# Cached keys and values of a head pair: load and split placed behind the pair's first key or value projection step

## The chip, the core and the metric

The kernel runs on one core of a Trainium2 chip. The metric is device time in microseconds (us) of one execution. The core has a matmul engine (TensorE, PE in the profile, with its weight loads as PEld), VectorE (DVE), ScalarE (ACT), GpSimd (POOL) and SyncE (SP), whose queue issues all the transfers of this kernel.

## The reference, cut to what matters

Two encoder layers are computed for 1024 prompt frames and 64 sample frames that share their weights. The sample frames also attend to 256 cached frames.

```python
# even layer, group B: 8 heads of chunk-band attention (group A is latent attention)
kb_all = jnp.concatenate([c_bk, k_b], 1); vb_all = jnp.concatenate([c_bv, v_b], 1)
o_b = _band_sample(q_b, kb_all, vb_all, c_bk.shape[1], table)
# odd layer: 16 heads of stick-breaking attention
q, k, v = _odd_project(x, w_in)
k_all = jnp.concatenate([c_k, k], 1); v_all = jnp.concatenate([c_v, v], 1)
o = _stick_breaking(q, k_all, v_all, pos, jnp.arange(k_all.shape[1]))
return o.reshape(B, T, MIX_C) @ w_out, k, v      # k and v are outputs too
# every layer: x <- LN(alpha*x + mixer(x)); x <- LN(alpha*x + sqrelu_mlp(x))
```

## The kernel before, in words

All products are made to float32 accuracy from two parts of each operand: `split` (L151) writes a high part H with ACT (L152) and the remainder L with DVE (L153); `mm3` then makes three matmuls (L157 to L159) for one product. Heads are handled in pairs, since a head has 64 features: four pairs of the band attention in the even layer, eight pairs in the odd one. `heads64` (L568) sets up one pair. Its nine steps project queries, keys and values for the token chunks 0:384, 384:768 and 768:1088, each with 24 matmuls into one PSUM bank ("d" or "s", two of each; from the second pair on only the two "d"). A key step is copied out of its bank by `split` for either head of the pair into the tile kS (64 partitions each), and by one more ACT copy (L618) into a tile `kraw`, which is stored to the output (L620). In the odd layer every key step has that copy, in the band layer only the steps from token 512 on; a value step has it always, and its `kraw` is then transposed and split into V (`put_values`, L538). The bank is free when the last of these copies has read it. `kraw` has two buffers, used in turn by all that asks for it.

The cached keys and values of the pair go the same way: a load into a `kraw` tile (L586 keys, L593 values, 128 KB), in the band layer a store of that tile to an output (L588, L595), and `split` into columns 1024:1280 of kS (one ACT and one DVE instruction for either head) or into blocks 8 and 9 of V (one of each). This stands at the head of the first "k" and the first "v" step, behind the load and split of the projection weight (`weight`, L183) and ahead of the 24 matmuls. The cached rows are read by the fifth of the nine work units of the pair's attention (`attend`, L813; `order` holds a pair (0, 4) there).

The attention of a pair runs beside the projection of the next: `paced` (L641) ties each projection step to a transpose of the running attention. In attention, scores (L655) go to a bank; in the odd layer ACT makes two sigmoids (L713, L714), DVE a scan (L720, L722) and POOL a product (L723); the weights are transposed (L175), split into wtH and wtL, and multiplied with V (L787, L789). The first pair of either layer has its nine steps ahead of any attention; in the odd layer they are taken in the order k0, q0, k1, q1, k2, q2, v0, v1, v2.

The order of the instructions in each engine's queue is not that of the source. The framework plans it ahead of time on a timeline of its own estimates: an instruction that stands earlier in the source has the higher priority, but one whose operands are planned to be ready is placed when its engine is free. On the chip each queue then runs in the planned order, and the head of a queue that waits for a semaphore holds up what stands behind it.

Of the kernel before, what the change touches and what calls it, by code (L numbers as in the profile page):

```python
# [13 lines left out]
P = 128  # L14
D = 1024
KD = D // P
SEQ = 1024
DEC = 64
T = SEQ + DEC
PAST = 256  # L20
# [24 lines left out]
def key_parts(c0, n):  # L45
    if c0 + n <= SEQ:
        return [(0, n, c0)]
    a = SEQ - c0
    return [(0, a, c0), (a, n - a, SEQ + PAST)]
# [74 lines left out]
class Net:  # L124
# [443 lines left out]
    def heads64(self, cp, bp, tiles, pair, w, cacheT, cache_v, outs, out0, cache_outs=(None, None), first=None, sooner=None, order=None):  # L568

        nc = self.nc
        qH, qL, qS, kS, V = tiles
        half = (slice(0, 64), slice(64, 128))
        feat = slice(pair * P, (pair + 1) * P)
        x = (self.xH, self.xL)
        ws = {}

        def step(kind, c0, n):
            if kind not in ws:
                ws[kind] = first if kind == "k" and first else self.weight(w[kind][pair], [P, KD, P], sooner)
                if kind == "k":
                    raw = self.tl(bp, [P, 384], "kraw", 2)
                    nc.sync.dma_start(raw[:, :PAST], cacheT[pair])  # L586
                    if cache_outs[0] is not None:
                        nc.sync.dma_start(cache_outs[0][feat, :], raw[:, :PAST])  # L588
                    for h in range(2):
                        self.split(kS[half[h], h, SEQ : SEQ + PAST], kS[half[1 - h], h, SEQ : SEQ + PAST], raw[half[h], :PAST])  # L590
                if kind == "v":
                    raw = self.tl(bp, [P, 2, P], "kraw", 2)
                    nc.sync.dma_start(raw, cache_v[:, feat].rearrange("(b p) c -> p b c", p=P))  # L593
                    if cache_outs[1] is not None:
                        nc.sync.dma_start(cache_outs[1][:, feat].rearrange("(b p) c -> p b c", p=P), raw)  # L595
                    self.split(V[:, 8:10, :, :64], V[:, 8:10, :, 64:], raw.rearrange("p b (h d) -> p b h d", h=2))
            ps = self.ps("d" if pair else "ds")
            mark = self.dense(ps[:, :n], ws[kind], x, KD, c0, n)
            if kind == "q":
                m = min(n, SEQ - c0)  # L600
                for h in range(2):
                    r, c = half[h], slice(c0, c0 + m)
                    self.split(qH[r, h, c], qL[r, h, c], ps[r, :m])
                    nc.scalar.activation(qH[half[1 - h], h, c], ps[r, :m], AF.Copy)
                    if m < n:
                        c = slice(h * DEC, h * DEC + DEC)
                        self.split(qS[r, h, 0, c], qS[r, h, 1, c], ps[r, m:n])
                        nc.scalar.activation(qS[half[1 - h], h, 0, c], ps[r, m:n], AF.Copy)  # L608
                return mark
            if kind == "k":  # L610
                for a, m, kc in key_parts(c0, n):
                    for h in range(2):
                        r, c = half[h], slice(kc, kc + m)
                        self.split(kS[r, h, c], kS[half[1 - h], h, c], ps[r, a : a + m])
            lo = max(c0, out0)
            if lo < c0 + n or kind == "v":
                raw = self.tl(bp, [P, 384], "kraw", 2)
                nc.scalar.activation(raw[:, :n], ps[:, :n], AF.Copy)  # L618
                if lo < c0 + n:
                    nc.sync.dma_start(outs[kind][feat, lo - out0 : c0 + n - out0], raw[:, lo - c0 : n])  # L620
                if kind == "v":
                    parts = [(i * P, min(P, n - i * P), (c0 // P + i) if c0 + i * P < SEQ else 10) for i in range(-(-n // P))]
                    self.put_values(V, raw, parts)
            return mark

        work = [(kind, c0, n) for kind in "kqv" for c0, n in CHUNKS]
        if order:
            work = [work[i] for i in order]
        steps = [lambda a=a: step(*a) for a in work]

        def score(h, i):

            if i < 8:
                st = [(x[:, h, i * P : i * P + P], kS[:, h, :]) for x in (qH, qL)]
            else:
                st = [(qS[:, e, x, :], kS[:, e, :]) for e in range(2) for x in range(2)]
            return lambda kc, n: self.scores([(a, k[:, kc : kc + n]) for a, k in st], n)

        return score, V, steps
# [1206 lines left out]
```

## Time and profile before

| | |
|---|---|
| time, median of 3 runs | 2795.22 us (2793.05 to 2797.9) |
| profiled execution: its time, its span | 2797.55 us, 2795.8 us |
| mean granted TensorE clock | 0.992 |
| busy share of the span: PE, DVE, ACT, POOL | 98%, 77%, 54%, 27% |
| band attention and its projections | about 177 to 400 us |
| first pair's projections of the odd layer | about 1428 to 1472 us |
| stick-breaking attention of the odd layer | about 1472 to 1955 us |

Busy times are those of one execution. A pause of PE that the profile lists has behind it, in brackets, its length and what ended it. Matmuls overlap, so the start-to-start distance of two matmuls, and not the duration of one, is what a matmul costs.

### The profile page before, as it was taken

The numbers are of one execution on the slowest core, as the hardware profiler recorded it, in microseconds if no ns is written. First come the engines' busy times: TensorE is split into PE (matmuls) and PEld (weight loads), VectorE is DVE, ScalarE is ACT, GpSimd is POOL, SyncE is SP. The second block draws the span as 40 slices with busy tenths as digits, with TensorE's granted clock in tenths as the row PEclk, the third lists the DMA queues.
The fourth block names the chain that finished last, engine by engine and source line by source line (L and its number), as shares of the span: only waits on it lengthen the run. The fifth ranks groups of instructions, "written<-read, shape, count | busy, mean of one in ns | idle before, by whom it ended". The sixth has DMA issues, their size and how long they took to land. (4 is left out here: it accounts for less than half of the span.)

```text
span 2795.8 us, 46944 instructions
## 1 busy us (share of the span) xinstructions
PE 2728.2 (98%) x16931; PEld 2496.0 (89%) x16931; DVE 2158.9 (77%) x3833; ACT 1511.5 (54%) x3103; POOL 745.6 (27%) x879
## 2 busy tenths in 40 slices
PE   9999999999999999999999999999999999999998
PEld 8999987888999998888789999998789999977786
DVE  4336777786867777999968887878787777789999
ACT  4235666873555556333257777777545555543331
POOL 3123334652100001221533343434330000022245
PEclk9999999989999999999999999999999999999999
DMA  7152234334234448444321111112252444763432
GB/s 216 49 168 60 73 97 100 87 108 149 93 131 139 162 143 268 131 139 138 111 91 58 51 54 52 54 51 80 77 168 100 161 131 138 242 189 120 150 122 87
DMA packets 226801, 331.33 MB, mean 119 GB/s; under 512 B 44489, under 2 KB 159241, under 8 KB 226505
## 3 DMA queue, kind: packets, MB, share of 16 engines
q1 hardware_dynamic: 226568, 328.34, 37.1%
q8 instruction: 134, 2.20, 0.3%
q14 instruction: 99, 0.80, 0.1%
HBM read 216.58 MB, written 109.99 MB: 117 GB/s over the span
## 5 line engine op out<-in xcount | busy, mean ns | idle before, releaser
L723 POOL TENSOR_TENSOR G<-G,S 128x384 f32<-128x384 f32 (+4 forms) x200 | 201.2, 1010 | 339.6 <-DVE S L720 121.2
L157 PE MATMUL d<-xH,wH 128*128 128x384 f32 (+1 forms) x784 | 262.6, 335 | 3.8 <-ACT qS L608 2.3
L159 PE MATMUL d<-xH,wL 128*128 128x384 f32 (+1 forms) x784 | 261.4, 333 | 0.0
L158 PE MATMUL d<-xL,wH 128*128 128x384 f32 (+1 forms) x784 | 260.1, 332 | 0.0
L153 DVE TENSOR_TENSOR wtL<-t,wtH 128x512 fp32r<-128x512 f32 (+2 forms) x328 | 196.9, 618 | 46.3 <-ACT wtH L152 37.5
L152 ACT ACTIVATE wtH<-t 128x512 fp32r<-128x512 f32 (+2 forms) x328 | 170.3, 545 | 47.9 <-PE t L175 21.3
L1493 POOL MEMSET sl<- 64x1024 f32 x2 | 1.9, 948 | 661.7 <-PE d L158 331.0
L787 PE MATMUL pv<-wtH,V 128*128 128x256 f32 (+1 forms) x624 | 159.2, 280 | 4.0 <-ACT o L747 2.8
L662 POOL TENSOR_TENSOR R<-R,inv 128x640 f32<-128x640 f32 (+6 forms) x100 | 115.5, 1167 | 174.8 <-DVE inv L661 103.5
L789 PE MATMUL pv<-wtL,V 128*128 128x256 f32 (+1 forms) x624 | 154.2, 288 | 7.5 <-DVE wtL L153 7.4
L157 PEld LDWEIGHTS d<-xH,wH 128*128 128x128 f32 x784 | 147.9, 189 | 8.1 <-ACT qS L608 3.2
L720 DVE TENSOR_TENSOR_SCAN S<-S,own 128x513 f32<-128x513 f32 (+3 forms) x144 | 144.3, 1012 | 11.9 <-ACT S L713 9.7
L158 PEld LDWEIGHTS d<-xL,wH 128*128 128x128 f32 x784 | 147.9, 189 | 1.3
L159 PEld LDWEIGHTS d<-xH,wL 128*128 128x128 f32 x784 | 147.7, 188 | 1.2
L152 ACT ACTIVATE wo<-wo 128x1024 fp32r<-128x1024 f32 (+4 forms) x92 | 79.7, 875 | 103.4 <-DMA wo<-o 24.9
L789 PEld LDWEIGHTS pv<-wtL,V 128*128 128x128 f32 x624 | 120.4, 193 | 11.3 <-DVE wtL L153 9.9
L787 PEld LDWEIGHTS pv<-wtH,V 128*128 128x128 f32 x624 | 120.1, 192 | 9.5 <-ACT o L747 5.6
L175 PE MATMUL t<-ident,G 128*128 128x128 f32 x600 | 103.3, 277 | 13.5 <-POOL S L711 7.7
L655 PE MATMUL s<-kS,qH 128*128 128x384 f32 (+3 forms) x288 | 105.7, 369 | 3.3 <-DVE mx L678 2.3
L713 ACT ACTIVATE S<-s 128x384 f32<-128x384 f32 (+4 forms) x200 | 98.7, 494 | 14.4 <-PE s L655 12.5
L714 ACT ACTIVATE G<-s 128x384 f32<-128x384 f32 (+4 forms) x200 | 99.5, 497 | 0.1
L655 PE MATMUL s<-kS,qL 128*128 128x384 f32 (+3 forms) x288 | 96.9, 338 | 0.0
(1817 smaller groups left out, 9906.3 us busy)
## 6 DMA issues: line engine op xcount, KB each, us to landing
sl<-a_d SPq DMA_DIRECT2D x37, 512.0 KB
wo<-a_d SPq DMA_DIRECT2D x36, 512.0 KB
a_d<-wo SPq DMA_DIRECT2D x31, 544.0 KB
wo<-in_w_dn SPq DMA_DIRECT2D x27, 512.0 KB
wo<-in_w_up SPq DMA_DIRECT2D x21, 512.0 KB
a_d<-sl SPq DMA_DIRECT2D x19, 544.0 KB
sl<-in_w_dn SPq DMA_DIRECT2D x20, 512.0 KB
sl<-in_w_up SPq DMA_DIRECT2D x17, 512.0 KB
```

The lines of the kernel that those rows point to most:

```text
L152: self.after(self.nc.scalar.activation(H, src, AF.Copy), mark)
L153: (engine or self.nc.vector).tensor_tensor(L, src, H.bitcast(F32), op=ALU.subtract)
L157: i = mm(out, aH, bH, start=first, stop=False)
L158: mm(out, aH, bL, start=False, stop=False)
L159: mm(out, aL, bH, start=False, stop=last)
L175: return self.nc.tensor.transpose(out, in_, self.ident[:n, :n])
L655: self.nc.tensor.matmul(ps[:, :n], q, k, start=i == 0, stop=i == len(passes) - 1)
L662: nc.gpsimd.tensor_tensor(R[:, :nk], R[:, :nk], inv.to_broadcast([P, nk]), op=ALU.mult)
L720: nc.vector.tensor_tensor_scan(s[r], s[r], own, carry, op0=ALU.mult, op1=ALU.max)
L723: nc.gpsimd.tensor_tensor(G[:, :n], G[:, :n], S[:, 1 : n + 1], op=ALU.mult)
L787: mm(out, v, wH[:, s : s + n], start=bi == 0 and s == 0, stop=False)
L789: mm(out, v, wL[:, s - n : s], start=False, stop=bi == len(banks) - 1 and j == bank[-1][0])
```

## The change

The load, the store and the split of the cached rows become a function `cached`. The step calls it behind its product instead of ahead of it, and only for the chunk that starts at token 0. Since `product` contains the copies out of the bank, the cached rows now stand behind the whole first key step (its splits, its L618 copy and its store), and behind the whole first value step (its L618 copy, its store and `put_values`). The amount of work is the same. The turn of the two `kraw` buffers changes: in an odd pair the uses were cached keys, k0, k1, k2, cached values, v0, v1, v2, and become k0, cached keys, k1, k2, v0, cached values, v1, v2.

```diff
+        def cached(kind):
+            if kind == "k":
+                raw = self.tl(bp, [P, 384], "kraw", 2)
+                nc.sync.dma_start(raw[:, :PAST], cacheT[pair])
+                if cache_outs[0] is not None:
+                    nc.sync.dma_start(cache_outs[0][feat, :], raw[:, :PAST])
+                for h in range(2):
+                    self.split(kS[half[h], h, SEQ : SEQ + PAST], kS[half[1 - h], h, SEQ : SEQ + PAST], raw[half[h], :PAST])
+            if kind == "v":
+                raw = self.tl(bp, [P, 2, P], "kraw", 2)
+                nc.sync.dma_start(raw, cache_v[:, feat].rearrange("(b p) c -> p b c", p=P))
+                if cache_outs[1] is not None:
+                    nc.sync.dma_start(cache_outs[1][:, feat].rearrange("(b p) c -> p b c", p=P), raw)
+                self.split(V[:, 8:10, :, :64], V[:, 8:10, :, 64:], raw.rearrange("p b (h d) -> p b h d", h=2))
+
         def step(kind, c0, n):
+            mark = product(kind, c0, n)
+            if c0 == 0:
+                cached(kind)
+            return mark
+
+        def product(kind, c0, n):
             if kind not in ws:
                 ws[kind] = first if kind == "k" and first else self.weight(w[kind][pair], [P, KD, P], sooner)
-                if kind == "k":
...
-                if kind == "v":
...
             ps = self.ps("d" if pair else "ds")
             mark = self.dense(ps[:, :n], ws[kind], x, KD, c0, n)
```

## Rows read from the trace of the kernel before

**Rows 1.** The page, busy time of each engine over the whole span.
```profile
PE 2728.2 (98%) x16931; PEld 2496.0 (89%) x16931; DVE 2158.9 (77%) x3833; ACT 1511.5 (54%) x3103; POOL 745.6 (27%) x879
```

**Rows 2.** Stretches: from:to, length, busy of PE, PEld, DVE, ACT, POOL, clock, DMA.
```profile
177.00:400.00 223.00, 220.20 (x1485) 217.66 (x1484) 139.31 (x437) 140.03 (x340) 73.56 (x87) 0.99 0.25 77
...
1490.00:1945.00 455.00, 439.07 (x2968) 422.54 (x2967) 380.41 (x550) 335.61 (x805) 179.74 (x347) 1.00 0.16 50
```

**Rows 3.** Waits of PE from 1440 to 1950: total us, times, longest us.
```profile
PE t L175 <- POOL S L711: 5.3, 9, 1.3
PE pv L789 <- DVE wtL L153: 5.1, 5, 1.1
PE d L157 <- ACT qS L608: 2.3, 3, 0.9
...
PE s L157 <- ACT kraw L618: 1.8, 1, 1.8
```

**Rows 4.** What touches kraw: durations min/median/max in ns, first and last start.
```profile
L153 DVE TENSOR_TENSOR kS<-kraw,kS x24: 407/420/747, 190.1 to 1886.9; 64x256 fp32r<-64x256 f32 x24
...
L153 DVE TENSOR_TENSOR V<-kraw,V x12: 391/426/1018, 201.2 to 1909.8; 128x256 fp32r<-128x256 f32 x12
```

**Rows 5.** Timeline of PE, first odd pair, every third matmul of k2: start, duration.
```profile
1447.37 0.41 PE L157 MATMUL s<-xH,wH 128*128 128x320 f32 x1 [1.81 <-ACT kraw L618]
...
1447.92 0.33 PE L157 MATMUL s<-xH,wH 128*128 128x320 f32 x1
...
1451.65 0.31 PE L157 MATMUL s<-xH,wH 128*128 128x320 f32 x1
...
1452.09 0.31 PE L157 MATMUL s<-xH,wH 128*128 128x320 f32 x1
```

**Rows 6.** Stretches of 2 us behind that pause, columns as in rows 2.
```profile
1448.00:1450.00 2.00, 2.00 (x10) 2.00 (x9) 0.56 (x1) 1.34 (x4) 0.23 (x4) 0.52 0.55 197
1450.00:1452.00 2.00, 2.00 (x11) 2.00 (x10) 0.00 (x0) 0.47 (x1) 0.00 (x0) 0.63 0.03 8
```

**Rows 7.** Timeline of ACT, the same place.
```profile
1443.68 0.86 ACT L152 ACTIVATE kS<-kraw 64x256 fp32r<-64x256 f32 x2 [0.31 <-DMA kraw<-in_cache_skT]
1444.56 0.49 ACT L152 ACTIVATE kS<-s 64x384 fp32r<-64x384 f32 x1
...
1446.85 0.47 ACT L618 ACTIVATE kraw<-s 128x384 f32<-128x384 f32 x1
```

**Rows 8.** Timeline of DVE, the same place.
```profile
1444.28 0.55 DVE L153 TENSOR_TENSOR kS<-s,kS 64x384 fp32r<-64x384 f32 x1
1444.76 0.86 DVE L153 TENSOR_TENSOR kS<-kraw,kS 64x256 fp32r<-64x256 f32 x2
1445.65 0.56 DVE L153 TENSOR_TENSOR kS<-s,kS 64x384 fp32r<-64x384 f32 x1
```

**Rows 9.** Timeline of SP: a load of the first odd pair, two stores of a later one.
```profile
1441.60 0.33 SPq L586 DMA_DIRECT2D kraw<-in_cache_skT  x1
...
1591.48 6.68 SPq L620 DMA_DIRECT2D o_svT<-kraw  x2
```

**Rows 10.** Timeline of DVE, cached keys of the third odd pair.
```profile
1548.27 0.75 DVE L153 TENSOR_TENSOR kS<-kraw,kS 64x256 fp32r<-64x256 f32 x1
1549.05 0.56 DVE L153 TENSOR_TENSOR wtL<-t,wtH 128x384 fp32r<-128x384 f32 x1
```

**Rows 11.** Timeline of PE, the same place.
```profile
1549.66 0.39 PE L789 MATMUL pv<-wtL,V 128*128 128x256 f32 x1 [0.80 <-DVE wtL L153]
```

**Rows 12.** Timeline of POOL, the same place.
```profile
1547.50 1.24 POOL L723 TENSOR_TENSOR G<-G,S 128x512 f32<-128x512 f32 x1 [1.25 <-DVE S L722]
```

**Rows 13.** Timeline of ACT, first band pair.
```profile
189.66 0.86 ACT L152 ACTIVATE kS<-kraw 64x256 fp32r<-64x256 f32 x2 [7.79 <-DMA kraw<-in_cache_bkT]
```

**Rows 14.** Stretches of one odd pair each, columns as in rows 2.
```profile
1540.00:1609.00 69.00, 65.27 (x436) 62.06 (x435) 56.26 (x83) 48.97 (x117) 26.91 (x51) 1.00 0.18 54
1609.00:1676.00 67.00, 65.33 (x445) 63.20 (x443) 57.82 (x83) 51.10 (x123) 26.58 (x52) 1.00 0.17 54
```

More of the change, by code (lines that the diff above doesn't have):

```diff
@@ L579, in heads64 @@
         ws = {}
-        def step(kind, c0, n):
+        def cached(kind):
[12 more added lines that the diff above has]
+                self.split(V[:, 8:10, :, :64], V[:, 8:10, :, 64:], raw.rearrange("p b (h d) -> p b h d", h=2))
+        def step(kind, c0, n):
+            mark = product(kind, c0, n)
[3 more added lines that the diff above has]
+        def product(kind, c0, n):
             if kind not in ws:
                 ws[kind] = first if kind == "k" and first else self.weight(w[kind][pair], [P, KD, P], sooner)
-                if kind == "k":
[L585 to L590, printed above, removed]
-                if kind == "v":
[L592 to L596, printed above, removed]
             ps = self.ps("d" if pair else "ds")
```

## The prediction

> **What bounds the kernel now.** The page's first part comes first: PE is busy 2728.2 us of 2795.8 us [rows 1]. So 67.6 us is all that any shift of work between the other engines can win at once, apart from a higher clock. The moved work lies in two stretches. Tabled as stretches, they show where PE stands still: in the band layer 223.00 - 220.20 = 2.8 us, in the stick-breaking layer from 1490 to 1945 us 455.00 - 439.07 = 15.9 us, with DVE at 380.41 of 455 us and ACT at 335.61 [rows 2]. PE sets the pace; DVE, five sixths full, is the engine that makes PE wait.
>
> The waits of PE say for whom: POOL's memsets, DVE's wtL, the query copies, and once, for 1.8 us, the copy L618 of a key step [rows 3]. No line names a cached load or split. The cached rows can therefore matter only as something that stands in a queue ahead of what PE waits for, and the timelines have to show where they do. The list for kraw gives their cost: 24 key pieces on DVE at 0.420 us and 12 value pieces at 0.426 us [rows 4], with ACT pieces of about the same length. That makes 24 moved groups, a key and a value group in each of 12 pairs.
>
> **The change part by part.** *First odd pair, where a moved group stands in front of PE.* Step k2 needs the bank of k0 and starts after a pause of 1.81 us, ended by k0's L618 [rows 5]. Behind the pause the granted clock is 0.52 and then 0.63 of full speed [rows 6], so part of the time is at the lower level of 1.2 GHz. The starts of k2's L157 show what that costs: from 1447.92 to 1451.65 five groups of three matmuls take 3.73 us, where the next group takes 0.44 us [rows 5], so 3.73 - 5 x 0.44 = 1.53 us are lost.
>
> L618 is late because the copies out of k0's bank alternate between ACT and DVE, and the cached keys stand between them on both. On ACT the two cached pieces (0.31 us of waiting for the load, then 0.86 us) precede the split of k0's second head at 1444.56 [rows 7]. On DVE the two cached pieces fill 1444.76 to 1445.62, and k0's second head follows at 1445.65 [rows 8]. With the cached pieces behind L618, ACT can begin that second head at 1443.68; DVE, at work on k1's first head until 1444.28 + 0.55 = 1444.83, then takes it for 0.56 us until 1445.4; and L618 follows, ending at about 1445.9 instead of 1446.85 + 0.47 = 1447.3. Gain 1.4 us. The pause left is 0.4 us. Pauses of up to 1.3 us are among those between 1490 and 1945 [rows 3], where the granted clock is 1.00 [rows 2], so I take the 1.53 us as won too. Bounds: nothing, if the planner fits the cached pieces into gaps of the same chain, and 1.81 + 1.53 = 3.3 us, if the whole pause goes. I take 1.4 + 1.5 = 2.9 us, since the removed work (1.17 us on ACT, 0.86 us on DVE) is in the chain itself.
>
> *The load.* Here it goes from issue at 1441.60 [rows 9] to its first use at 1443.68 [rows 7] in 2.08 us. In an odd pair the load moves past one issue of SP, k0's store (keys) or v0's store (values), each about 0.33 us; what stands behind it, weight loads above all, is later by no more than the wait for that copy. The fifth attention unit, first to read the cached rows, belongs to the next pair period, some 67 us on. I cost it at nothing. If that cover were gone it would cost its 2.08 us.
>
> *The turn of the kraw buffers.* k1 now takes k0's buffer and waits for its store to land. With the load's 2.08 us for a store, k1's copy cannot start before 1445.9 + 2.1 = 1448.0; its bank is next wanted by v0, behind k2 and q2 of 8 x 0.44 = 3.5 us each, from 1446 on, so at 1453. v1 likewise takes over v0's buffer two uses later; in a later pair two value stores are issued within 6.68 us [rows 9], against 2.08 us for landing plus the transposes of v0. Nothing; bound 2.1 us at the first pairs, whose steps have no attention between them.
>
> *The other 22 odd and band groups beside this pair's.* Their work (two pieces or one of 0.42 us on either engine) is the same before and after; only its neighbours differ. Of these groups one stops PE in the trace: the third odd pair's second key piece ends at 1549.02, the split wtL follows [rows 10] and PE has waited 0.80 us for it [rows 11]. That pause may go, and another may come. I take one such pause before and one after, so 0; bounds -0.8 us and, if each group met a wtL, 22 x 0.80 = +17.6 us. Where a group is hidden it is hidden under PE's matmuls, and costs 0.80 us when it is not.
>
> That piece took 0.75 us instead of 0.42 us, and ran while POOL multiplied from 1547.50 to 1548.74 [rows 12]. The Trainium skill (page SBUF — State Buffer, section Who interferes with whom) says that a VectorE instruction with two SBUF inputs contends with a GpSimd instruction that reads SBUF; the trace agrees here, with 0.33 us more. By that rule the copies out of a bank are spared and the cached pieces are not, so that a piece moved onto a POOL product would add an estimated 0.33 us to a pause; by the rows alone the price stays 0.80 us.
>
> *First band pair.* ACT waits 7.79 us at the head of its queue for the cached load [rows 13], ahead of k0's second head. It looks like the largest prize. But the band stretch holds 2.8 us of PE pauses in all, and none is ended by this: four banks serve this pair. Gain 0.
>
> *Sum.* -1.4 - 1.5 = -2.9 us: against the profiled execution 2797.55 - 2.9 = 2794.65 us. That execution lies 2.33 us above the median of the three runs, so the forecast is 2795.22 - 2.9 = 2792.3 us. Below, 0.2% of the time, 5.6 us, is what a measurement can tell from no change.
>
> **The rivals.**
>
> *Nothing moves.* Queue order is planned by readiness. If the cached pieces are planned into the same gaps as now, the time is 2795.2 us. For it: two buffers of kraw are free at the start of the odd layer, so the load can still be planned at 1441.6. Against it: in ACT's queue the cached pieces would have to precede a split that is ready by the same moment and now has priority.
>
> *A better rhythm.* Odd pairs alternate: 69.00 - 65.27 = 3.7 us of pauses in one, 67.00 - 65.33 = 1.7 us in the next [rows 14]. If that holds for the six pairs from 1540 on, three are long, and they could become short if later cached pieces and earlier L618 copies unload DVE at the right moment: 3 x 2.0 = 6 us more, 2795.2 - 2.9 - 6 = 2786.3 us. For it: the pauses are DVE's, and banks are freed sooner. Against it: the largest part of the pauses, 5.3 us, is ended by POOL's memsets [rows 3], which the change doesn't touch.
>
> *Slower: cached pieces ahead of wtL.* At their new place the pieces hold up wtL as in the third pair, 0.80 us each time. With all seven later odd pairs and three band pairs hit by their keys it is 10 x 0.8 - 2.9 = +5.1 us, 2800.3 us; from (5.6 + 2.9) / 0.8 = 11 groups on it is measurably slower, with all 22 it is 2809.9 us. For it: DVE is at 380 of 455 us. Against it: it happens in 1 of 22 now.
>
> **How the numbers follow.** The forecast has 0.38, nothing moves 0.18, the better rhythm 0.27, slower 0.17. The first two lie within 0.2%, but the forecast can miss it by a little: faster 0.29, same 0.54, slower 0.17. The range from 2785.5 to 2800.5 us takes in the better rhythm with a margin of 0.8 us and the ten hits; the likeliest case alone spans 2790 to 2795 us.
>
> **What would show it.** In the first odd pair: L618 of k0 ahead of the pieces from kraw on ACT and DVE, k2's pause under 0.8 us, granted clock 1.00 from 1448 to 1452. In the later pairs: the waits of PE for wtL at about the 5.1 us of now. In the first band pair: ACT's long wait gone or moved, with PE unchanged. The prediction is wrong if k2's pause stays (planned gaps), if PE's waits for wtL or for POOL change by more than 3 us over the odd layer, or if the projections wait for kraw buffers.

## The result and the profile after

The changed kernel takes 2808.88 us (median of 4 runs, 2806.34 to 2813.55) against 2794.75 us before, measured on the same chip. The ratio is 1.005, with a 95% interval of 1.0038 to 1.0062. The forecast was 2792.3 us with a range up to 2800.5 us: the change is slower by 14 us, where no change or a gain of 3 us was expected. The profiled execution spans 2811.8 us. In the changed kernel the lines behind the edit are numbered nine higher: L618 is now L627, L711 L720, L714 L723, L723 L732, L655 L664, L789 L798.

The span is 16.0 us longer, but PE is busy only 6.3 us longer than in [rows 1], and it does the same products: most of the loss has to be found in its pauses. The page's first part:

```profile
PE 2734.5 (97%) x16931; PEld 2499.0 (89%) x16931; DVE 2163.2 (77%) x3833; ACT 1509.0 (54%) x3103; POOL 752.1 (27%) x879
```

The two stretches of [rows 2] again, from the view of stretches (PE, PEld, DVE, ACT, POOL busy, granted clock, DMA share, GB/s). The odd layer begins 6.0 us later here (memset of `own` at 1447.6 instead of 1441.6 us), so the second stretch holds slightly earlier work than in [rows 2]:

```profile
177.00:400.00 223.00, 219.54 (x1472) 216.78 (x1472) 139.41 (x435) 140.03 (x337) 73.27 (x87) 0.99 0.26 78
1490.00:1945.00 455.00, 433.04 (x2887) 413.59 (x2886) 379.43 (x540) 326.26 (x788) 173.63 (x336) 1.00 0.16 49
```

In the stick-breaking stretch PE now pauses 455.00 - 433.04 = 22.0 us instead of 15.9 us and gets through 2887 matmul records instead of 2968. The waits of PE from 1440 to 1950 us (total us, times, longest) say for whom:

```profile
PE d L157 <- ACT kraw L627: 6.8, 7, 1.2
PE s L664 <- ACT G L723: 4.2, 4, 1.3
PE t L175 <- POOL G L732: 4.0, 9, 0.7
PE t L175 <- POOL S L720: 2.7, 5, 1.3
PE pv L798 <- DVE wtL L153: 2.5, 3, 1.4
PE t L175 <- DVE V L153: 0.9, 2, 0.4
PE s L157 <- ACT kraw L627: 0.6, 1, 0.6
```

The first line is new: a projection step waits for the copy L627 out of a bank, seven times about 1 us. From 1480 to 1960 us this line was 0.8 us in two waits before. The waits for POOL's memsets and for wtL, which led [rows 3], have halved. Those for POOL's product G and for ACT's second sigmoid (G L723), which frees a bank of scores, have grown, from 2.0 to 4.0 and from 0.9 to 4.2 us. The last line is the pause of the first pair, 1.8 us in [rows 3] and 0.6 us now.

Here is one of the seven, in the fifth odd pair's projection. Timelines of PE, ACT and DVE (start, duration, line, what; in brackets the idle time ahead of it and what ended it); the rows of each engine stand together:

```profile
1700.46 0.45 PE L157 MATMUL d<-xH,wH 128*128 128x384 f32 x1 [0.97 <-ACT kraw L627]
...
1693.61 0.86 ACT L152 ACTIVATE kS<-kraw 64x256 fp32r<-64x256 f32 x2
...
1694.90 0.49 ACT L152 ACTIVATE kS<-d 64x384 fp32r<-64x384 f32 x1
...
1698.34 0.49 ACT L152 ACTIVATE kS<-d 64x384 fp32r<-64x384 f32 x1 [2.20 <-DVE kS L153]
1699.92 0.49 ACT L627 ACTIVATE kraw<-d 128x384 f32<-128x384 f32 x1 [1.09 <-DVE kS L153]
...
1695.62 1.66 DVE L153 TENSOR_TENSOR kS<-kraw,kS 64x256 fp32r<-64x256 f32 x2
...
1697.75 0.55 DVE L153 TENSOR_TENSOR kS<-d,kS 64x384 fp32r<-64x384 f32 x1
1698.33 0.96 DVE L729 TENSOR_TENSOR_SCAN S<-S,own 128x385 f32<-128x385 f32 x1
1699.33 0.56 DVE L153 TENSOR_TENSOR kS<-d,kS 64x384 fp32r<-64x384 f32 x1
```

k0's copies are over; k1's have to empty the second of two "d" banks. ACT splits k1's first head at 1694.90, but DVE has the two cached pieces in front and takes the counterpart at 1697.75. ACT, whose next split waits for DVE, stands idle 2.20 and 1.09 us; L627 comes at 1699.92, and step q0, which needs that bank, starts 0.97 us late. The two pieces take 1.66 us rather than 2 x 0.42 us [rows 4], while POOL multiplies from 1695.75 to 1696.99. A small addition of the attention (0.42 us) and a scan (0.96 us) stand in the same DVE chain.

Only one other of the seven is of this kind, at 1840.09 us (0.99 us): together 1.96 of the 6.8 us. In four others, 4.34 us, step q1 waits for the copies of k2, 18 to 19 us behind ACT's cached pieces, when both engines have long been done with them; the last, 0.53 us, is a later step's. The first of the four:

```profile
1711.33 0.44 PE L157 MATMUL d<-xH,wH 128*128 128x384 f32 x1 [1.18 <-ACT kraw L627]
...
1710.84 0.44 ACT L627 ACTIVATE kraw<-d 128x320 f32<-128x320 f32 x1 [1.03 <-DVE kS L153]
```

In front of DVE's parts of these copies stand scans, splits of the attention weights and the split of a projection weight. How the moved pieces bring them to this place was not followed.

### The profile page after: what moved, and what is told of

Read it like the earlier page. It is cut to its first block, busy times and chain, and to the rows that moved or that the text cites. A ratio compares the mean times of both kernels' runs of the same rounds, so it can differ in the third digit from the quotient of the medians.

```text
span 2811.8 us, 46906 instructions
## 1 busy us (share of the span) xinstructions
PE 2734.5 (97%) x16931; PEld 2499.0 (89%) x16931; DVE 2163.2 (77%) x3833; ACT 1509.0 (54%) x3103; POOL 752.1 (27%) x879
## 5 line engine op out<-in xcount | busy, mean ns | idle before, releaser
L732 POOL TENSOR_TENSOR G<-G,S 128x384 f32<-128x384 f32 (+4 forms) x200 | 204.7, 1026 | 344.5 <-DVE S L729 146.8
L798 PE MATMUL pv<-wtL,V 128*128 128x256 f32 (+1 forms) x624 | 154.8, 289 | 5.7 <-DVE wtL L153 5.6
L798 PEld LDWEIGHTS pv<-wtL,V 128*128 128x128 f32 x624 | 120.8, 194 | 9.2 <-DVE wtL L153 7.7
L664 PE MATMUL s<-kS,qH 128*128 128x384 f32 (+3 forms) x288 | 104.9, 367 | 12.8 <-ACT G L723 6.7
L723 ACT ACTIVATE G<-s 128x384 f32<-128x384 f32 (+4 forms) x200 | 100.3, 502 | 2.2 <-PE t L175 2.2
L731 DVE TENSOR_TENSOR_SCAN S<-S,S 128x385 f32<-128x385 f32 (+1 forms) x64 | 93.8, 1466 | 7.7 <-ACT S L722 3.5
```

Of the source, the lines that this page charges most:

```text
L664: self.nc.tensor.matmul(ps[:, :n], q, k, start=i == 0, stop=i == len(passes) - 1)
L732: nc.gpsimd.tensor_tensor(G[:, :n], G[:, :n], S[:, 1 : n + 1], op=ALU.mult)
L798: mm(out, v, wL[:, s - n : s], start=False, stop=bi == len(banks) - 1 and j == bank[-1][0])
```

## The experiments

All kernels but e8, e10 and e13, which keep the old place, share one edit of the changed kernel; `late` says which groups stand behind the first step, and every other group stands where it stood before. All of them compute the whole reference.

```diff
-            if c0 == 0:
+            if c0 == 0 and late(kind):
                 cached(kind)
...
                 ws[kind] = first if kind == "k" and first else self.weight(...)
+                if kind != "q" and not late(kind):
+                    cached(kind)
```

The columns: median in us; ratio to the kernel before with its interval; waits of PE for the copy out of a "d" bank in the stick-breaking pairs; from the memset of `own`, with which this layer begins, to its last projection product; from there to its last score. The three right-hand columns are read from the one profiled execution.

| kernel | median | ratio | bank waits | to last product | then to last score |
|---|---|---|---|---|---|
| before | 2794.75 | | 0.8 | 500.5 | 63.7 |
| changed | 2808.88 | 1.0050 [1.0038, 1.0062] | 6.8 | 510.6 | 63.9 |
| e1 even layers only | 2798.62 | 1.0011 [1.0001, 1.0020] | 0.8 | 498.7 | 63.1 |
| e2 odd layer only | 2807.27 | 1.0043 [1.0028, 1.0058] | 6.9 | 509.7 | 65.4 |
| e3 odd keys | 2801.81 | 1.0023 [1.0014, 1.0033] | 6.0 | 502.4 | 67.3 |
| e4 odd values | 2792.15 | 0.9992 [0.9983, 1.0002] | 0 | 496.4 | 66.5 |
| e5 odd pair 0 | 2794.43 | 1.0002 [0.9993, 1.0011] | 0.8 | 498.4 | 65.1 |
| e6 odd pairs 1 to 6 | 2808.99 | 1.0056 [1.0042, 1.0070] | 5.9 | 512.3 | 66.1 |
| e7 odd pair 7 | 2793.24 | 1.0000 [0.9990, 1.0009] | 1.0 | 498.8 | 65.2 |
| e8 heads swapped | 2793.57 | 0.9999 [0.9990, 1.0008] | 0.8 | 497.3 | 63.7 |
| e9 odd keys, on POOL | 2790.42 | 0.9985 [0.9976, 0.9994] | 0 | 491.4 | 66.8 |
| e10 late last step | 2800.68 | 1.0021 [1.0011, 1.0032] | 1.0 | 506.2 | 63.4 |
| e11 one even group | 2797.46 | 1.0009 [1.0001, 1.0018] | 0.8 | 498.8 | 63.1 |
| e12 values and first keys | 2791.87 | 0.9989 [0.9981, 0.9998] | 0 | 493.8 | 66.0 |
| e13 before, on POOL | 2793.35 | 0.9994 [0.9985, 1.0003] | 0.8 | 498.3 | 65.2 |
| e14 odd layer, on POOL | 2787.91 | 0.9979 [0.9969, 0.9989] | 0.4 | 490.9 | 65.8 |

**The change in halves.** e1: `late = not odd`; e2: `late = odd`; e3: `odd and kind == "k"`; e4: `odd and kind == "v"`.

> Cached rows stand behind the first projection step only in the band and MLA layers; in the stick-breaking layer they stand as before. In the trace of the changed kernel the even layers end 5 to 6 us later than before (first memset of the odd layer at 1447.6 instead of 1441.6 us). Theory A (two separate costs, one at the seam of the two even layers and one in the odd pairs): +5 to +6 us, about 2800.5. Theory B (planner noise that comes back later): the loss at the seam is made up in the odd layer, 2794 to 2797. Theory C (all of the loss is in the odd layer): no change, 2795.

> The other half: cached rows behind the first step only in the stick-breaking layer. Theory A: the changed kernel's own odd part, -3 us at the first pair, +10 us over the steady pairs, +3 to +6 us at the last pair, so +8 to +11 us, about 2804. Theory B (the odd loss follows from the odd layer's later start, not from the order of its copies): within 3 us of the kernel before, or 3 us faster.

> Only the cached keys of the odd layer stand behind the first key step; its cached values stand as before. Theory K (the cached key pieces sit between the copies of the first and the second key bank, of two banks, so that each steady pair pays about 1 us of waits for the copy out of a bank): -3 at the first pair and 6 to 7 us of such waits over the later ones, so +3 to +6 us, about 2799.5. Theory V (the value groups, whose load now waits for a kraw buffer, carry the loss): -3 us, about 2792.

> Only the cached values of the odd layer stand behind the first value step; its cached keys stand as before. Theory K (keys carry the loss): within 2 us of the kernel before. Theory V (value loads wait for the kraw buffer and ACT waits at the head of its queue for them): +6 to +12 us, most of it in the later pairs and at the last one, about 2804.

The halves add up: 3.6 us from the even layers and 12.2 us from the odd one, 15.8 us against 14.1 us measured (differences of medians). Theory A holds and B falls, but the 5 to 6 us read from the single trace were too much for the even half. Within the odd layer the keys carry 6.8 us, with 6.0 us of bank waits. The values alone cost nothing, so theory V falls, yet with the keys they make it 12.2 us: more than the sum.

**Which pairs.** e5: `odd and pair == 0`; e6: `odd and 0 < pair < 7`; e7: `odd and pair == 7`. e8 leaves everything in the old place and only swaps the two heads of the cached key split:

```diff
-                for h in range(2):
+                for h in (1, 0):
                     self.split(kS[half[h], h, SEQ : SEQ + PAST], ...
```

> Cached keys and values behind the first step only in the first pair of the stick-breaking layer, where no attention runs yet; all other pairs and layers as before. Theory F (the gain of the first pair is real, and the loss is made in the pairs with attention between the steps): in the two half changes the first late unit of this layer came 2.2 us earlier by the keys and 3.7 us earlier by the values, so 5 to 6 us faster, about 2789.5. Theory N (any change of the order reshuffles the whole layer by some us either way): anything from -6 to +6, and a first-pair gain that the later pairs undo.

> Keys and values behind the first step in pairs 1 to 6 of the stick-breaking layer, not in pair 0 (before any attention) and not in pair 7 (the last). Theory T1 (steady pairs pay: the cached key split stands between the copies of the first two key steps, and the product that wants the bank waits for the copy to kraw): the pairs between the first and the last late unit lose about 9 us, waits of PE for that copy 5 to 6 us in all, so +8 to +10 us, about 2804. Theory T5 (the loss is the last transition): +2 or less.

> Keys and values behind the first step only in pair 7 of the stick-breaking layer, whose projection ends just before the output projection's weights are loaded. Theory T5 (the last projection ends later, so that the loads and splits of the output weights fall on an attention that DVE and POOL already bound): +5 to +7 us, about 2801, with the last attention period long. Theory T1 (every pair pays about 1 to 2 us): +1 to +2 us. Theory A2 (delay carried over from earlier pairs): 0.

> A neutral reordering of the kernel before: the cached keys stay ahead of the first key step, only the second head's half is split ahead of the first head's, in all pairs of both layers. No work is added and no load moved. Theory N (order noise of the planned queues is worth some us by itself): a time off by 3 us or more either way. Otherwise within 2 us of the kernel before, and the 6 to 12 us of the other kernels have a cause in the place of the group.

Neither pair 0 nor pair 7 changes the time (the 5 to 6 us that theory F expected of e5 did not come); pairs 1 to 6 make all of the odd loss, 14.4 us. Theory T5, as put, falls: the last projection is not late because of its own groups.

e8 shows less than it was meant to: in its trace the order of PE's 16,931 matmuls, by tiles and sizes, is that of before, so it only swaps two pieces on ACT and DVE. What a replanned order is worth by itself it can't show. e4 and e12 change PE's order in about 2,290 places, as e3 does in 2,250, and come out 3 us faster instead of 7 us slower. So a new order need not cost anything, but a few us of any of these differences can be chance of the plan.

The loss of e6 up to the last projection is 512.3 - 500.5 = 11.8 us, of which only 23.2 - 17.5 = 5.7 us are pauses of PE (sums over the timeline, e6 and before, up to the last product). In the other 5.8 us (488.6 - 482.8 us) PE counts as busy. A part of it is attention work done ahead of that product: 7 transposes and 8 products with V more than before, an estimated 7 x 0.087 + 8 x 0.117 = 1.5 us by the mean start-to-start distances of the two kinds in this part of the layer before. The other 4.3 us are the same matmuls at longer distances, transposes above all; why was not followed. Counted over PE's timeline, the last value step starts 5,632 columns of scores, transposes and products with V later in e6 and 5,760 in the changed kernel, in e2 and in e10, but 1,152 and 1,024 columns earlier in e3 and e4 (the expectations have other counts).

**The late last step, by itself.** e10 keeps all groups in the old place and ties only the last projection to a mark one unit later:

```diff
-            self.paced(steps, marks, 2 if pair < 7 else -3)
+            self.paced(steps, marks, -3 if pair == 7 else 1 if pair == 6 else 2)
```

> The kernel before with all cached rows in their old place; only the steps of the last projection (pair 7) are tied to a mark of the attention one unit later, so that the last value step stands 5,504 score, weight and transpose columns later in PE's queue, as it does in the kernel with pairs 1 to 6 moved (5,504) and in the changed kernel (5,312). Theory S (from the last projection product to the last score the time is 63 to 67 us in every kernel so far, however much attention was done by then, so work done ahead of that product is not given back): +5 to +7 us, about 2801. Theory T1 (all of the loss is bank waits): no change.

It costs 5.8 us, as expected: 506.2 - 500.5 = 5.7 us to the last product, and from there 63.4 us as before. In the trace the 5.7 us are 2.0 us more pauses and 486.5 - 482.8 = 3.7 us more busy time; of the latter 10 transposes and 8 products with V are an estimated 1.8 us, and a second fall of the clock (0.50 for 3.4 us from 1898.4) up to 1.7 us. So a late step costs more than the work done ahead of it. That this work isn't given back either is seen in the stretch that follows the last product. From the stretches of before, changed and e10, in this order:

```profile
1942.00:2006.00 64.00, 54.64 (x318) 47.22 (x317) 58.83 (x72) 45.21 (x95) 29.58 (x48) 0.95 0.43 138
```
```profile
1958.00:2022.00 64.00, 54.34 (x296) 46.03 (x296) 57.18 (x69) 42.68 (x88) 31.58 (x45) 0.89 0.43 138
```
```profile
1944.00:2008.00 64.00, 54.70 (x294) 45.63 (x293) 56.14 (x67) 43.18 (x91) 27.09 (x45) 0.89 0.43 137
```

PE has 22 to 24 matmuls fewer here, but needs the same 64 us. It stands still for 9 to 10 us of them, and is busy as long as before at a mean clock of 0.89 instead of 0.95, which is 13.7 instead of 6.8 us at 0.50; DVE is the fullest engine, at 56 to 59 us. Which of the two, the clock or DVE, holds the stretch at 64 us was not separated. In this stretch the weights of the output projection are loaded into the space that the last projection frees (first load at 1947.6 us before, 5 us behind the last product), and their splits fall on DVE beside the last attention.

**The bank waits, by themselves.** e9 is e3 with the subtraction of the cached odd keys on POOL from pair 1 on; e13 is the kernel before with this edit alone; e14 is e2 with it.

```diff
                     self.split(kS[half[h], h, SEQ : SEQ + PAST], ...
-                               raw[half[h], :PAST])
+                               raw[half[h], :PAST], nc.gpsimd if out0 == 0 and pair else None)
```

> As the kernel with only the stick-breaking keys moved (6.4 to 6.8 us slower than before, waits of PE for the copy out of a key bank 6.0 us in 7 pauses), but from pair 1 on the second half of the cached key split, the subtraction, is done by POOL instead of DVE. Theory T1 (on DVE the cached pieces stand between the copies of the first and the second key bank, and that is what holds the bank): the waits for the copy out of the bank fall from 6.0 us to about 1 us, and the time to between +0 and +2 us, about 2796. Theory T1-ACT (the cached pieces on ACT alone hold the bank): the waits stay near 6 us, about 2801. If POOL is the next bound, the waits for its products and memsets grow by more than the 5 us won: 2801 or more.

> The kernel before, cached rows in their old place, with the subtraction of the cached stick-breaking keys on POOL from pair 1 on. Theory P (the 4.5 us that the kernel with moved keys on POOL is faster come from DVE having 14 pieces less, wherever the group stands): -3 to -5 us, about 2791. Theory T1 (they come from the place: behind the first step the group is harmless once it doesn't stand in DVE's queue between two bank copies): within 1.5 us of the kernel before.

> All cached keys and values of the stick-breaking layer behind the first step (12.2 us slower than before with all pieces on DVE), with the subtraction of the cached keys on POOL from pair 1 on. The last value step then stands 1,600 columns later in PE's queue than before, instead of 5,312. Theory T1 plus S (bank waits plus the late last projection are all of the 12 us): the bank waits fall to about 1 us and a quarter to a third of the slip's 6 us stays, so 0 to +3 us, about 2796. If the moved values had a cost of their own beside moved keys (their loads wait for a kraw buffer): +5 us or more, above 2800.

In e9 the waits for L627 (L633 there) are gone from the steady pairs; the waits of PE from 1480 to 1960 us now begin so:

```profile
PE t L175 <- POOL S L726: 5.1, 5, 2.2
PE t L175 <- POOL G L738: 4.9, 4, 2.8
PE pv L804 <- DVE wtL L153: 3.8, 3, 1.4
PE t L175 <- DVE wtL L153: 3.1, 6, 0.9
```

With this one edit the kernel goes from 2801.81 to 2790.42 us and the bank waits of the steady pairs go with the pieces on DVE, while ACT's pieces stay; T1-ACT falls. The same edit in the old place gains 0.8 us by the medians, not told from nothing (e13), so the 11 us don't come from unloading DVE as such. But the waits that went are 6.0 us. The edit also changes PE's order against e3 in 1,784 of 16,931 places (e13 against before in 6), so the other 5 us may be the new plan's. e14 settles the open point: both groups late, with the keys' pieces off DVE, are 6.2 us faster than before, better than the 0 to 3 us slower that was expected. So the moved values have no cost of their own. Beside keys on DVE they make the last product late: e2 reaches it 7.3 us after e3, and PE is busy 5.6 us longer (488.3 against 482.7 us). An estimated 2.0 us of that is attention work done ahead (12 transposes, 8 products with V), and up to 3.4 us are two falls of the clock to 0.50 for 3.4 us each in e2's trace, of which e3's has none. In e14 that step is 1,024 columns late instead of 5,760. Why the planned order lets it slip when both groups move, and not when one does, stays open. e14 beats both kernels. POOL pays for it: its pieces last 1.22 us in the median in e14, 0.73 us in e13, where they stand elsewhere (durations in ns, min/median/max):

```profile
L153 POOL TENSOR_TENSOR kS<-kraw,kS x12: 728/1222/1542, 1543.8 to 1877.3; 64x256 fp32r<-64x256 f32 x12
```
```profile
L153 POOL TENSOR_TENSOR kS<-kraw,kS x12: 728/732/1532, 1541.4 to 1881.3; 64x256 fp32r<-64x256 f32 x12
```

**The even half, and a mixed version.** e11: `not odd and kind == "v" and pair == 1`; e12: `odd and (kind == "v" or pair == 0)`.

> In the even layers only one group moved: the cached values of the second band pair; all else as before. The queues from there on differ from those of before nearly as much as with all even groups moved, while the moved key groups of the band layer leave every queue as it was. Theory E (the even loss is a changed order further on, not the moved work): the same +3 us as with all even groups, 2797 to 2799, most of it where the first output weights are split. Theory W (each moved group costs its own share): below +1 us.

> In the stick-breaking layer the values of all pairs and the keys of the first pair behind the first step; all other groups as before. The last value step stands 1,920 columns earlier in PE's queue than before. Theory T1 plus S: the keys of the later pairs carry the loss and are left out, so -2 to -4 us, about 2792. Theory N (order noise): anything within 5 us of the kernel before.

One moved value group of 0.4 us on either engine costs 2.6 us, nearly as much as all eight groups of the even layers. That speaks for theory E, but with intervals too wide to tell 2.6 from 3.6 us, or from W's 1 us: it is 0.3 to 5 us. The key groups of the band layer leave every queue in the same order. Where the loss arises isn't shown. The place that theory E names, the split of the first output weights, has longer pauses in e11, one of them 2.20 us, but a higher clock. The same 85 us in e11 and before:

```profile
618.75 0.79 PE L159 MATMUL d<-wo,wo 128*128 128x512 f32 x1 [2.20 <-DVE wo L153]
```
```profile
560.00:645.00 85.00, 76.15 (x475) 66.64 (x474) 64.41 (x177) 61.04 (x135) 41.34 (x43) 0.94 0.33 97
```
```profile
560.00:645.00 85.00, 80.36 (x473) 69.87 (x472) 63.58 (x168) 59.94 (x133) 39.81 (x42) 0.90 0.33 97
```

PE pauses 8.85 against 4.64 us and still gets through 475 against 473 matmuls. By the memset of `own` the even layers take 1442.6 us in e1, 1443.9 in e11 and 1447.6 in the changed kernel; in the 12 profiled kernels whose even layers are those of before it is 1436.8 to 1442.3 us, so one execution each can't place 3 us. e12 is 3 us faster than before, as expected.

## Why the prediction was wrong

*First odd pair: right in the trace, too small to be measured.* The cached pieces now stand behind L627, and k2's pause went from 1.81 us [rows 5] to 0.65 us. Timelines of PE and ACT, and two stretches behind the pause:

```profile
1452.20 0.42 PE L157 MATMUL s<-xH,wH 128*128 128x320 f32 x1 [0.65 <-ACT kraw L627]
...
1451.65 0.49 ACT L627 ACTIVATE kraw<-s 128x384 f32<-128x384 f32 x1
...
1452.93 0.84 ACT L152 ACTIVATE kS<-kraw 64x256 fp32r<-64x256 f32 x2
```
```profile
1452.80:1454.80 2.00, 2.00 (x15) 2.00 (x14) 1.21 (x3) 1.92 (x5) 1.59 (x8) 1.00 0.28 98
1454.80:1456.80 2.00, 2.00 (x16) 2.00 (x15) 0.56 (x1) 1.86 (x3) 0.00 (x0) 1.00 0.32 103
```

That is 1.2 us of the 1.4 us worked out, and the clock is 1.00. But the 1.5 us for the clock could not be counted on: of the nine profiled kernels that keep a pause of 1.66 to 1.81 us there, three (before, e6, e10, with the longest pauses, 1.76 to 1.81 us) show the drop and six don't. In the changed kernel a drop of the same length comes later, at 1630 us, behind a pause of 1.34 us. e5, this step alone with the pair's values, has a ratio of 1.0002. A drop seen in one execution was taken for a property of the kernel.

*The load and the turn of kraw: right at nothing.* ACT waits for cached value loads at the head of its queue, but no wait of PE goes back to one. The copies out of the banks wait for DVE's splits, never for a store of kraw. A third kraw buffer was not tried, since it doesn't fit beside the others.

*The other 22 groups: the step that failed.* It priced a group that meets something only at what a piece had done to wtL, 0.80 us, took one such hit before and one after, and so came to 0. "Only its neighbours differ" was true; the neighbours were the fault. Behind the first key step the cached pieces stand in front of k1's copies, and with two banks q0 can't start until those are done. In the old place they stood ahead of k0's copies, while PE was still at work on k0. The prediction had read just this chain in the first pair, where it counted the release of k0's bank as a gain, and did not ask which bank's copies would now stand behind the pieces. In the place of its 0, e6 measured 14.4 us for pairs 1 to 6. The changed kernel's bank waits grew from 0.8 to 6.8 us in seven places, and go with the pieces on DVE (e9, e14); only 1.96 us of them are this chain read directly, and the way to the other five is open. The one meeting with wtL that the prediction knew stayed what it was, 0.88 us at 1555.11 us against 0.80 us [rows 11].

*The missing term.* No step asked what becomes of the end of the layer when the order of the steps changes. The last value step starts 5,760 columns later in PE's order, and e10, with the same slip, shows its price alone: 5.8 us. Up to the last projection product the changed kernel has 22.1 - 17.5 = 4.6 us more pauses and 488.0 - 482.8 = 5.2 us more busy time, of which an estimated 1.8 us are 18 matmuls done ahead; the 64 us behind it didn't shrink. The clock has a share in it that no run separates: the mean granted clock of the changed kernel's four executions is 0.991, that of 31 of the kernel before 0.993. If PE had been busy throughout, the difference (0.9908 against 0.9926) would be an estimated 5 us; yet e9, at a mean of 0.991 too, is faster than before.

*First band pair: right.* ACT still waits at the head of its queue, and PE doesn't mind:

```profile
191.35 0.86 ACT L152 ACTIVATE kS<-kraw 64x256 fp32r<-64x256 f32 x2 [8.19 <-DMA kraw<-in_cache_bkT]
```

The even layers' loss of about 3 us, put at 0, comes with the value group of the second pair alone, as far as e11's interval tells.

*The rivals.* "Slower" had the sign and the wrong mechanism: the waits for wtL fell from 5.1 to 2.5 us [rows 3]. Its condition, DVE at five sixths, was the right reason for concern. Gains of the kind of "a better rhythm" come in e14 and e12 once the later keys are out of DVE's way, 6 and 3 us: PE's pauses up to the last product fall from 17.5 to 11.2 and 13.7 us. Whether alternate pairs became even was not looked at.

Two cached pieces of 0.42 us each [rows 4] took 1.66 us while POOL multiplied, 0.8 us more in a chain that ends in a wait of 0.97 us. The Trainium skill (page SBUF — State Buffer, section Who interferes with whom) says that a VectorE instruction with two SBUF inputs contends with a GpSimd instruction that reads SBUF; the trace agrees. For the waits on k2's copies it shows nothing, since the pieces are done by then.

## What to carry to other kernels

Before moving work behind a step, name the buffer that this step fills, count its copies of the pool, and list whose emptying will now stand behind the moved work in each queue; off the critical path is not enough where two banks alternate. Look at the stretch where the layer ends: if it takes the same time however much is done before, a last step that slips is paid for (5.8 us here). What lies between two such copies may go to an engine that doesn't take part in them (e9, e14). And where a plan reorders thousands of instructions, test the size of what order alone can do with a kernel whose order really differs.

## What the runs showed of the hardware

A pause of PE is followed by a lower clock in some executions and not in others. Behind the first pair's pause it is so before, behind 1.81 us, and not in e8, behind 1.72 us (the stretch of 5 us, then the pause):

```profile
1447.60:1452.60 5.00, 5.00 (x25) 5.00 (x25) 0.93 (x2) 2.20 (x6) 0.57 (x6) 0.66 0.23 82
```
```profile
1446.40:1451.40 5.00, 5.00 (x36) 5.00 (x35) 1.59 (x3) 3.53 (x7) 0.58 (x6) 1.00 0.24 82
...
1446.09 0.41 PE L157 MATMUL s<-xH,wH 128*128 128x320 f32 x1 [1.72 <-ACT kraw L633]
```

25 against 36 matmuls in 5 us, at a mean of 0.66 and of 1.00: part of the first stretch ran at the lower level, 1.2 GHz. There the pauses differ by 0.09 us. A pause of one length, ended by the same instruction, shows both outcomes in e2 and in e6:

```profile
1619.49 0.45 PE L670 MATMUL s<-kS,qH 128*128 128x384 f32 x1 [1.32 <-ACT G L729]
...
1619.40:1624.40 5.00, 4.55 (x16) 4.14 (x17) 4.76 (x6) 4.97 (x12) 2.80 (x4) 0.66 0.11 39
```
```profile
1621.26 0.45 PE L670 MATMUL s<-kS,qH 128*128 128x384 f32 x1 [1.32 <-ACT G L729]
...
1621.20:1626.20 5.00, 4.58 (x27) 4.17 (x28) 4.75 (x6) 4.98 (x12) 2.81 (x4) 1.00 0.11 39
```

16 against 27 matmuls behind 1.32 us. At the first pair's place none of the seven profiled kernels with the pause cut to 0.65 us (changed, e2, e3, e5, e9, e12, e14) shows a drop; beside three in nine, that is too few to call the shorter pause safe.
